# First-layer attention: three pairs of PSUM banks, one projection bank emptied by a copy, and a held TensorE order

## The chip, the cores and the metric

The kernel runs on one core of one Trainium2 chip. Its metric is the device time of one execution in microseconds (us): the median of three runs before the change is 1449.96 us (1449.54 to 1451.34). The engines of the core are TensorE (PE, with its weight loads shown apart as PEld), VectorE (DVE), ScalarE (ACT), GpSimd (POOL) and SyncE (SP), which issues the DMAs. Data lie in SBUF; TensorE writes its results to PSUM, which has eight banks of 512 float32 values for each of the 128 partitions. POOL takes no part in reading PSUM here.

## The reference, cut to what matters

Two layers over 1024 latent tokens and 256 context tokens, 1024 wide, 16 heads of 64. The first layer is windowed attention with rotary position and a sink logit for each head, a SiLU gate, an output projection and a LayerNorm; the second layer is a two-dimensional neighbourhood attention with the same frame. The change is in the first layer:

```
q, k, v, g = split(u @ w_in)             # u: tokens after adaLN; 4 key/value heads, 16 query heads
q, k = rope(q), rope(k)                  # latent tokens only
s = q . k / 8 over a block of 128 queries and its previous, own and next block, masked to |i-j| <= 128
p = softmax([s_window, s_context, sink])
o = p @ [v_window, v_context]
y = (o * silu(g)) @ w_out
h = layer_norm(sqrt(2) * h + gate * y)
```

Context queries attend to the context alone.

## The kernel before, in words

All products of float32 are kept exact enough by splitting operands into a high and a low part (`hi`, `lo`), so a projection of one 128-row weight tile onto 512 tokens is three matmuls (lines 208 to 210).

The first layer works on pairs of heads, p = 0 to 7. For each pair `subsA` lists 20 steps: ten blocks of 128 queries (8 of latents, 2 of context), each for two heads. Step k has these pieces of TensorE work:

- S (`qkA`, lines 694 to 716): the scores of step k + 3, four matmuls (two for context blocks) into one pair of PSUM banks, name `S_A`. VectorE adds the mask and takes the extreme (line 317, `m_A`), which frees that pair; ScalarE takes the exponential (324); VectorE inverts the sum (328); POOL normalises (329).
- T (`trA`, `sm_transpose`, line 336): up to five transpositions of step k's probabilities into another pair of banks, name `T_A`. ScalarE copies the high part (340), VectorE subtracts the low part (342), which frees that pair.
- V (`pvA_fn`, line 733): probabilities times values, in a first (high) and a second (low) half, into one bank, name `pvA`.

Before the change, PSUM is one pool: tag "big" with two pairs of banks, which S and T share, whichever is free, and tag "one" with four single banks, which the projections (`pj`) and `pvA` share.

While the attention of pair p runs, TensorE also computes the projections of the gate of pair p and of q of pair p + 1 (`proj_pieces`): for each, three chunks of tokens (512, 512, 256), each in eight pieces of three matmuls into one bank `pj`. At a chunk's last piece the bank is read by `evac`. For the gate (`g_evac`) that is a tanh on ScalarE (line 277) and a product on VectorE (278). For q (`rope_evac`) it is, for the two latent chunks, a shuffle (469) and a product with the cosine (470) on VectorE, a product with the sine on POOL (471), a sum on VectorE (472) into the one buffer "ra", and then for each of two heads a ScalarE cast (659) and a VectorE subtraction (660) that read "ra". The context chunk of q is stored from the bank itself by lines 659 and 660.

`merge` interleaves the two lists by their costs: it takes a projection piece whenever the projections' share done is not ahead of the attention's, so at the start of a pair (both zero) it takes a projection piece. `att_steps` sets the order of pieces within a step: T, S, V. This is the order in which the program is traced. A planner then gives each engine its order: it takes what is ready first in its own model of time, by priority; `lift(n)` raises the priority of what it encloses, and `keep_in_program_order` ties an instruction behind the one traced before it on its engine, without a wait.

Around it: `k_load` brings the keys of a group of two pairs as two tiles, with three buffers in all; q of pair 0 is computed alone before the attention (line 808); pair 7 has no q to fill with, and takes the output weights and the first output product (lines 824 to 848). Between them run the dot products of a modulation row (`dot_half`).

Of the kernel before, what the change touches and what calls it, by code (L numbers as in the profile page):

```python
# [19 lines left out]
P = 128  # L20
# [15 lines left out]
AHEAD_B, LIFT_B = 3, 40  # L36
BARE_B = 108
# [45 lines left out]
def build(tc, i, out):  # L83
    nc = tc.nc
    mm = nc.tensor.matmul
# [104 lines left out]
    def proj_pieces(j0, u, chunks, evac):  # L190
# [4 lines left out]
        def piece(ci, t0, n, kq):  # L195
# [18 lines left out]
            return (3 * 0.425 * n, run)  # L214
# [69 lines left out]
    def merge(att, fill, lead=0.0):  # L284

        ta = sum(a[0] for a in att) or 1.0
        tf = sum(f[0] for f in fill)
        ia = jf = 0
        ca = cf = 0.0
        while ia < len(att) or jf < len(fill):  # L290
            need = att[ia][2] if ia < len(att) and len(att[ia]) > 2 else 0
            if jf < len(fill) and (ia == len(att) or jf < need or cf - lead <= ca * (tf - lead) / ta):
                cf += fill[jf][0]
                fill[jf][1]()
                jf += 1
            else:
                ca += att[ia][0]
                att[ia][1]()
                ia += 1
# [31 lines left out]
    def sm_transpose(s, order, pt, hl, name):  # L331
# [3 lines left out]
        for k, src in enumerate(order):  # L335
            nc.tensor.transpose(tp[:, k * P : (k + 1) * P], s.t[:, src * P : (src + 1) * P], ident)  # L336
# [264 lines left out]
    def dot_half(h, j):  # L601
        def run():
# [13 lines left out]
            o = ap_.tile([P, 512], F32, tag="ra", bufs=1, name="gj")  # L616
# [29 lines left out]


# [45 lines left out]

    def qkA(k):
        p, b, h = subsA[k]
        q = qA[2 * p + h]
        sc = psbig(f"S_A{k}")
        ql = q[:, b * P : (b + 1) * P]
        n = len(tilesA(b)) * P - 256
        for l in range(2):  # L700
            kk = kA[p // 2, l]
            if n:
                t0 = tilesA(b)[0] * P
                mm(sc[:, 512 - n : 512], ql, kk[:, t0 : t0 + n], start=l == 0, stop=l == 1)
            mm(sc[:, 512:768], ql, kk[:, S:T], start=l == 0, stop=l == 1)  # L705
# [103 lines left out]
    px, px_st = pool("attA2", "right")  # L809
# [529 lines left out]
```

## Time and profile before

| what | value |
|---|---|
| median of three runs | 1449.96 us (1449.54 to 1451.34) |
| the profiled execution, its own time | 1450.25 us |
| its span, first to last instruction | 1448.5 us |
| granted TensorE clock, mean | 0.994 |
| TensorE busy | 1393.6 us, 96% |
| VectorE, ScalarE, POOL busy | 988.8, 733.9, 631.7 us |
| first S of the first layer | 98.1 us |
| last V of the first layer | 588.6 us |

The page gives for each engine the time in which it ran instructions. A row of a group names the line, the engine, the operation, what is written and read, and the count, then busy time and mean duration in ns, then the idle time of the engine before these instructions and what ended it. A row of waits says which engine, tile and line waited, for which engine, tile and line, and then the total in us, the number of waits and the longest. A timeline row gives the start in us from the start of the span, the duration, the engine and the instruction, with how many like it follow in the group (x5).

### The profile page before, as it was taken

The page shows a single profiled execution, that of the slowest core. Times are in us where ns is not written, and L with a number is a line of the kernel's source. Part 1 is how long each engine was busy: PE and PEld are TensorE (multiplying, and loading weights), DVE is VectorE, ACT ScalarE, POOL GpSimd, SP SyncE. Part 2 cuts the span into 40 slices and gives each one's busy share as a digit, 9 for nine tenths or more (in the row PEclk, how much of TensorE's full clock was granted, in tenths as well). Part 3 has the DMA queues.
Part 4 walks back from the last instruction along what each step waited for, and adds up shares of the span by engine and source line. Part 5 has one row for each costly group of instructions (what it writes and reads, how often), then busy time and mean ns, then how long its engine had stood idle before and what let it go on. Part 6 is the DMA issues. An engine that isn't in the chain of part 4 may idle for free. (4 is left out here: it accounts for less than half of the span.)

```text
span 1448.5 us, 25148 instructions
## 1 busy us (share of the span) xinstructions
PE 1393.6 (96%) x8815; PEld 1217.2 (84%) x8816; DVE 988.8 (68%) x2216; ACT 733.9 (51%) x1561; POOL 631.7 (44%) x779
## 2 busy tenths in 40 slices
PE   8998999999999999999999999999999999998995
PEld 5887888888888888788888899888988898887775
DVE  4658887878888789566423766555565565667698
ACT  4336776677676778332222545554454444557310
POOL 0326666666666657233301333333233333336664
PEclk9999999999999999999999999999999999999998
DMA  9472114123222124434278565565555564384353
GB/s 369 172 227 85 60 48 131 45 77 101 68 70 62 56 67 131 133 129 136 75 216 230 156 195 152 150 166 146 168 147 152 146 182 140 102 207 151 114 133 93
DMA packets 117229, 195.05 MB, mean 135 GB/s; under 512 B 9328, under 2 KB 57840, under 8 KB 117104
## 3 DMA queue, kind: packets, MB, share of 16 engines
q1 hardware_dynamic: 117104, 193.45, 44.4%
q8 instruction: 70, 1.15, 0.3%
q14 instruction: 55, 0.45, 0.1%
HBM read 141.51 MB, written 51.90 MB: 134 GB/s over the span
## 5 line engine op out<-in xcount | busy, mean ns | idle before, releaser
L329 POOL TENSOR_SCALAR s_B<-s_B,rs_B 128x640 f32<-128x640 f32 (+1 forms) x128 | 101.1, 790 | 298.0 <-DVE rs_B L328 243.9
L208 PE MATMUL pj<-uBh,wh 128*128 128x512 f32 (+1 forms) x448 | 176.0, 393 | 0.0
L209 PE MATMUL pj<-uBl,wh 128*128 128x512 f32 (+1 forms) x448 | 170.3, 380 | 0.0
L210 PE MATMUL pj<-uBh,wl 128*128 128x512 f32 (+1 forms) x448 | 170.1, 380 | 0.0
L324 ACT ACTIVATE s_B<-s_B,m_B 128x640 f32<-128x640 f32 (+1 forms) x128 | 102.9, 804 | 131.2 <-DVE m_B L317 131.1
L324 ACT ACTIVATE s_A<-s_A,m_A 128x641 f32<-128x641 f32 (+2 forms) x160 | 119.5, 747 | 88.7 <-DVE m_A L317 73.7
L164 POOL TENSOR_TENSOR wl<-wr,wh 128x512 fp32r<-128x512 f32 x64 | 87.7, 1370 | 162.1 <-ACT wh L162 139.8
L329 POOL TENSOR_SCALAR s_A<-s_A,rs_A 128x640 f32<-128x640 f32 (+2 forms) x160 | 126.8, 793 | 58.0 <-DVE rs_A L328 55.7
L317 DVE CUSTOM_DVE_ANT_0 s_A<-S_A,msk,nsk 128x640 f32<-128x640 f32 (+2 forms) x160 | 123.6, 774 | 34.1 <-PE S_A L705 17.7
L342 DVE TENSOR_TENSOR pt_B<-T_B,pt_B 128x640 fp32r<-128x640 f32 (+1 forms) x128 | 100.9, 788 | 61.0 <-ACT pt_B L340 60.6
L208 PE MATMUL pj<-uAh,wh 128*128 128x512 f32 (+1 forms) x384 | 140.0, 365 | 0.0
L209 PE MATMUL pj<-uAl,wh 128*128 128x512 f32 (+1 forms) x384 | 137.8, 359 | 0.0
L210 PE MATMUL pj<-uAh,wl 128*128 128x512 f32 (+1 forms) x384 | 137.5, 358 | 0.0
L342 DVE TENSOR_TENSOR ptl_A<-T_A,pth_A 128x640 fp32r<-128x640 f32 (+2 forms) x160 | 114.0, 713 | 15.3 <-PE pvA L733 7.1
L336 PE MATMUL T_A<-ident,s_A 128*128 128x128 f32 x672 | 101.1, 275 | 12.2 <-DVE m_A L317 8.9
L336 PEld LDWEIGHTS T_A<-ident,s_A 128*128 128x128 f32 x672 | 77.2, 140 | 40.2 <-issue 16.7
L340 ACT CAST pt_B<-T_B 128x640 fp32r<-128x640 f32 (+1 forms) x128 | 84.3, 658 | 47.6 <-PE T_B L336 46.6
L317 DVE CUSTOM_DVE_ANT_0 s_B<-S_B,bias 128x640 f32<-128x640 f32 (+1 forms) x128 | 100.4, 784 | 10.5 <-PE S_B L1036 9.7
L340 ACT CAST pth_A<-T_A 128x640 fp32r<-128x640 f32 (+2 forms) x160 | 96.4, 603 | 16.8 <-PE T_A L336 14.1
L210 PEld LDWEIGHTS pj<-uBh,wl 128*128 128x128 f32 x448 | 84.3, 188 | 16.6
L336 PE MATMUL T_B<-ident,s_B 128*128 128x128 f32 x608 | 88.7, 275 | 9.9 <-DVE pt_B L342 5.0
L242 PE MATMUL pv<-wh,uBh 128*128 128x256 f32 x320 | 92.8, 291 | 3.1 <-ACT wh L162 3.1
(219 smaller groups left out, 3883.6 us busy)
## 6 DMA issues: line engine op xcount, KB each, us to landing
kB<-kdB SPq DMA_DIRECT2D x64, 320.0 KB, 5.2
gw<-in_wadaT SPq DMA_DIRECT2D x48, 256.0 KB, 2.8
vdB<-st SPq DMA_DIRECT2D x20, 512.0 KB, 3.2
vB<-vdB SPq DMA_DIRECT2D x16, 640.0 KB, 4.7
wada<-in_wadaC SPq DMA_DIRECT2D x16, 512.0 KB, 9.6
kdB<-st SPq DMA_DIRECT2D x16, 512.0 KB, 3.0
qdB<-st SPq DMA_DIRECT2D x16, 512.0 KB, 3.5
qB<-qdB SPq DMA_DIRECT2D x32, 256.0 KB, 4.7
```

What stands on the lines that cost most here:

```text
L164: e.tensor_tensor(lo, r, f32(hi), ALU.subtract)
L208: mm(pt[:, :n], hi[:, sl], rh, start=kt == 0, stop=False)
L209: mm(pt[:, :n], hi[:, sl], rl, start=False, stop=False)
L210: mm(pt[:, :n], lo[:, sl], rh, start=False, stop=kt == KT - 1)
L242: mm(pt, lh, hi[:, sl], start=kt == 0, stop=False)
L317: nc.vector.tensor_tensor_reduce(outp, sc, in1, scale, init if init is not None else 3e38, ALU.add, ALU.min, accum_out=s.m)
L324: nc.scalar.activation(s.t[:, :n], s.t[:, :n], AF.Exp, bias=s.m, scale=-1.0, accum_out=s.sum)
L329: nc.gpsimd.tensor_scalar(s.t[:, : s.w], s.t[:, : s.w], s.rs, 1.0, ALU.mult, ALU.mult)
L336: nc.tensor.transpose(tp[:, k * P : (k + 1) * P], s.t[:, src * P : (src + 1) * P], ident)
L340: nc.scalar.copy(pt.hi[:, :n, hl, :], tv)
L342: nc.vector.tensor_tensor(pt.lo[:, :n, hl, :], tv, f32(pt.hi[:, :n, hl, :]), ALU.subtract)
```

## The change

Six edits, all around the first layer:

1. PSUM becomes a sequence of three pools: as before up to the first projections (two pairs, four singles), then for the first layer three pairs and two singles, one for `pj` and one for `pvA`, then two pairs and four singles again after the first output block. Pairs are taken strictly in turn by the traced order, each its own tag with one buffer, in all three pools.
2. The projections of q and of the gate are emptied by a copy on ScalarE, with the priority raised by `LIFT_PJ` = 40: q into "ra" (all three chunks, the context chunk too), the gate into its own tile `gA`. The rest of the work then reads the copy.
3. In `merge`, after the last piece of a first-layer chunk no projection piece is taken until attention pieces of cost 1700 have been.
4. From pair 0 up to and without pair 7 every matmul and transposition is tied behind the one traced before it.
5. For the first two steps of pairs 2, 4 and 6 the scores are issued in two parts: the part with the high keys at its place, the part with the low keys at the end of the second step.
6. The dot products write their unused result to "rb" instead of "ra", and the first output product of pair 7 takes the third pair (`big2`) instead of two single banks; from there the pairs in turn are two.

```
+LIFT_PJ = 40
+GAP_PJ = 1700.0
...
-    mm = nc.tensor.matmul
+    pinned = []
+    def pin(ins):
+        if pinned:
+            tc.keep_in_program_order(ins)
+    def mm(*a, **kw):
+        pin(nc.tensor.matmul(*a, **kw))
...
-    ps = es.enter_context(tc.tile_pool(name="ps", bufs=1, space=PSUM))
-    def psbig(name):
-        return ps.tile([P, 1024], F32, tag="big", bufs=2, name=name)
-    def psone(name):
-        return ps.tile([P, 512], F32, tag="one", bufs=4, name=name)
+    class Banks:
+        def open(self, name, pairs, ones):
+            self.st = ExitStack()
+            self.ps = self.st.enter_context(tc.tile_pool(name=name, bufs=1, space=PSUM, reuse_waits="tile"))
+            self.pairs, self.ones, self.n = list(range(pairs)), ones, 0
+        def big(self, name):
+            t = self.pairs[self.n % len(self.pairs)]
+            self.n += 1
+            return self.ps.tile([P, 1024], F32, tag=f"big{t}", bufs=1, name=name)
+        def one(self, name):
+            if self.ones == 4:
+                return self.ps.tile([P, 512], F32, tag="one", bufs=4, name=name)
+            return self.ps.tile([P, 512], F32, tag=name[:2], bufs=1, name=name)
+    banks = Banks()
+    banks.open("ps0", 2, 4)
+    psbig, psone = banks.big, banks.one
...
-            return (3 * 0.425 * n, run)
+            return (3 * 0.425 * n, run, GAP_PJ) if kq == 7 and j0 < NA else (3 * 0.425 * n, run)
...
-    def g_evac(pl, g):
+    def g_evac(pl, g, free=False):
         def evac(pt, t0, n):
+            if free:
+                pt, src = g[:, t0 : t0 + n], pt
+                with lift(LIFT_PJ):
+                    nc.scalar.copy(pt, src[:, :n])
             th = pl.tile([P, 512], F32, tag="ra", bufs=1, name="th")
...
-        ca = cf = 0.0
+        ca = cf = hold = 0.0
...
-            if jf < len(fill) and (ia == len(att) or jf < need or cf - lead <= ca * (tf - lead) / ta):
+            if jf < len(fill) and (ia == len(att) or jf < need or (ca >= hold and cf - lead <= ca * (tf - lead) / ta)):
                 cf += fill[jf][0]
                 fill[jf][1]()
+                if len(fill[jf]) > 2:
+                    hold = ca + fill[jf][2]
                 jf += 1
...
-    def rope_evac(store, pl, bufs):
+    def rope_evac(store, pl, bufs, free=False):
         def evac(pt, t0, n):
+            if t0 < S or free:
+                a = pl.tile([P, 512], F32, tag="ra", bufs=bufs, name="ra")
+            if free:
+                with lift(LIFT_PJ):
+                    nc.scalar.copy(a[:, :n], pt[:, :n])
+                pt = a
             if t0 >= S:
                 store(pt[:, :n], t0, n)
                 return
-            a = pl.tile([P, 512], F32, tag="ra", bufs=bufs, name="ra")
...
-            o = ap_.tile([P, 512], F32, tag="ra", bufs=1, name="gj")
+            o = ap_.tile([P, 512], F32, tag="rb", bufs=1, name="gj")
...
+    banks.st.close()
+    banks.open("psA", 3, 2)
...
-        return proj_pieces(pos["Aq", p], uA, CHUNKS, rope_evac(q_store(p), ap_, 1))
+        return proj_pieces(pos["Aq", p], uA, CHUNKS, rope_evac(q_store(p), ap_, 1, True))
...
-            g_evac(ap_, gA[p])(pt, t0, n)
+            g_evac(ap_, gA[p], True)(pt, t0, n)
...
     def qkA(k):
+        qk_part(k, 0)
+        if not (k >= 40 and k % 40 < 2):
+            qk_part(k, 1)
+    def qk_part(k, l):
...
+        if l == 0:
+            scA[k] = psbig(f"S_A{k}")
+        sc = scA[k] if l == 0 else scA.pop(k)
...
     merge([], qprojA(0))
     px, px_st = pool("attA2", "right")
+    pinned.append(True)
     for p in range(8):
-        att = [x for row in rowsA[p * 20 : (p + 1) * 20] for x in row]
+        rows_p = [list(row) for row in rowsA[p * 20 : (p + 1) * 20]]
+        if p == 7:
+            pinned.clear()
+        elif p % 2 == 0 and p:
+            late = range(p * 20, p * 20 + 2)
+            rows_p[1] += [(270.0, lambda k=k: qk_part(k, 1), 0) for k in late]
+        att = [x for row in rows_p for x in row]
...
-                yA0.extend(psone(f"yA0_{nh}") for nh in range(2))
+                banks.pairs = [0, 1]
+                y = banks.ps.tile([P, 1024], F32, tag="big2", bufs=1, name="yA0")
+                yA0.extend(y[:, sl] for sl in HALVES)
...
+        if b == 0:
+            banks.st.close()
+            banks.open("psB", 2, 4)
```

More of the change, by code (lines that the diff above doesn't have):

```diff
@@ L335, in sm_transpose @@
         for k, src in enumerate(order):
-            nc.tensor.transpose(tp[:, k * P : (k + 1) * P], s.t[:, src * P : (src + 1) * P], ident)
+            pin(nc.tensor.transpose(tp[:, k * P : (k + 1) * P], s.t[:, src * P : (src + 1) * P], ident))
         tv = tp[:, : n * P].rearrange("p (k q) -> p k q", k=n)
@@ L848, in build @@
             merge(att[-6:], [])
+    pinned.clear()
     px_st.close()
@@ L1241, in build @@
             dma(grid_rows(out, b)[:, :, sl], z[:, sl])
+    banks.st.close()
     ob_st.close()
```

18 lines of the change are left out of this document (9 added, 9 removed).

## The prediction

> **What bounds the kernel now.** I read the page first: TensorE's share of the span and the granted clock.
>
> ```profile
> span 1448.5 us, 25148 instructions
> ...
> PE 1393.6 (96%) x8815; PEld 1217.2 (84%) x8816; DVE 988.8 (68%) x2216; ACT 733.9 (51%) x1561; POOL 631.7 (44%) x779
> ```
>
> TensorE is busy nearly all the time. The profiled execution took 1450.25 us, 0.29 above the median of 1449.96; my sum starts at 1450.25. Next comes the table by stage of the changed stretch: pair 0 of the heads, pairs 1 to 6, and pair 7 with its tail. After the stretch and its length stand the busy us (and instructions) of TensorE, its weight loads, VectorE, ScalarE and POOL, then the granted clock, DMA share and GB/s.
>
> ```profile
> 98.00:158.00 60.00, 55.07 (x355) 47.72 (x353) 47.97 (x114) 39.47 (x89) 38.04 (x54) 1.00 0.35 99
> 158.00:525.00 367.00, 356.66 (x2318) 312.93 (x2319) 300.31 (x732) 255.81 (x584) 239.74 (x346) 1.00 0.24 74
> 525.00:595.00 70.00, 65.24 (x412) 56.45 (x411) 56.24 (x129) 51.26 (x110) 41.22 (x59) 1.00 0.34 106
> ```
>
> The shown idle time of TensorE is 4.93 + 10.34 + 4.76 = 20.0 us. The waits of TensorE say what ends it; the first three rows are of the whole kernel, the fourth of 525 to 595 us alone.
>
> ```profile
> PE T_A L336 <- DVE m_A L317: 8.9, 16, 1.6
> PE S_A L704 <- DVE ptl_A L342: 5.1, 7, 1.2
> PE S_A L705 <- DVE ptl_A L342: 1.8, 6, 0.3
> ```
> ```profile
> PE T_A L336 <- DVE m_A L317: 3.2, 5, 1.5
> ```
>
> A transposition (T) needs its scores from POOL, yet it waits for the minimum that VectorE takes of other scores (L317); scores (S) need only q and k, yet wait for VectorE's read of a transposition (L342). So both wait for a pair of banks: S and T share two. The timeline at the boundary from pair 1 to pair 2 of heads shows two such waits, and three things more.
>
> ```profile
> 216.11 0.28 PE L208 MATMUL pj<-uAh,wh 128*128 128x256 f32 x1
> 216.23 0.28 PE L209 MATMUL pj<-uAl,wh 128*128 128x256 f32 x1
> 216.34 0.28 PE L210 MATMUL pj<-uAh,wl 128*128 128x256 f32 x1
> 216.46 0.40 PE L208 MATMUL pj<-uAh,wh 128*128 128x512 f32 x1
> 216.70 0.40 PE L209 MATMUL pj<-uAl,wh 128*128 128x512 f32 x1
> 216.93 0.40 PE L210 MATMUL pj<-uAh,wl 128*128 128x512 f32 x1
> 217.48 0.41 PE L336 MATMUL T_A<-ident,s_A 128*128 128x128 f32 x2 [0.15 <-DVE m_A L317]
> 218.56 0.39 PE L704 MATMUL S_A<-kA,qA 128*128 128x256 f32 x1 [0.67 <-DVE ptl_A L342]
> ```
>
> First, a 128x512 matmul is drawn 0.40 long but the next starts 0.23 later, so each wait hides about 0.16 us more than its row says. The three rows hold 15.8 us in 29 waits, truly about 15.8 + 29 x 0.16 = 20.4. Second, the gate projection of pair 2 (216.46, 512 wide) follows directly on the last matmul of the query projection (216.34, 256 wide): no attention lies between. The merge makes it so at the start of each pair, because with both sums at zero its test takes a projection piece first. Third, that costs nothing now, since the projections have several banks.
>
> **The change, part by part.**
>
> *Third pair.* The waits of 98 to 525 us are (15.8 - 3.2) + 24 x 0.16 = 16.4, those of the tail 4.0, of which the third pair lives only in the first half: 2.0. With three pairs in turn a pair comes back after one and a half steps instead of about one. VectorE works 300.31 of 367 us (82%), so some lateness stays: I take 17 of the 18.4 as gone, with 10 as the lower bound (VectorE stays the last to answer).
>
> *The copies.* Each projected chunk gets a ScalarE copy: 8 x 3 for q, 8 x 3 for the gates. The nearest rows are the reads of the same bank for the second layer and for q's context columns.
>
> ```profile
> L932 ACT CAST st<-pj 128x512 fp32r<-128x512 f32 x16 | 9.4, 586 | 18.5 <-PE pj L210 13.0 <-issue 4.2 <-ACT otmp L1073 1.0
> L659 ACT CAST qA<-pj 64x256 fp32r<-64x256 f32 x16 | 5.8, 361 | 3.9 <-DVE qA L660 3.9
> L472 DVE TENSOR_TENSOR ra<-ra,rb 128x512 f32<-128x512 f32 x20 | 18.1, 903 | 1.1 <-POOL rb L471 0.8
> L470 DVE TENSOR_TENSOR ra<-pj,cos 128x512 f32<-128x512 f32 x16 | 10.8, 672 | 0.0
> ```
>
> 32 x 0.586 + 16 x 0.361 = 24.5 us of ScalarE, which is busy 255.81 of 367 (70%) and goes to about 76%: covered by TensorE's own work, so nothing by itself. VectorE's cosine product now reads two SBUF operands, like L472: up to 0.23 more on 16 instructions, 3.7 us, also covered while VectorE has 18% free; without that cover it would add at most those 3.7.
>
> *One projection bank, inside a pair of heads.* The hold of 1700 puts four attention pieces (4 x 545) between chunks, 35 times over pairs 0 to 6. Four full pieces are about 0.6 us each, 2.3 together; with the short blocks at a pair's end 1.5. The bank must be read meanwhile. A late case of today:
>
> ```profile
> 226.69 0.39 PE L210 MATMUL pj<-uAh,wl 128*128 128x512 f32 x1
> ```
> ```profile
> 228.39 0.59 ACT L277 ACTIVATE th<-pj 128x512 f32<-128x512 f32 x1
> ```
>
> ScalarE came 1.31 us after the bank was complete (227.08) and would free it 0.16 + 1.31 + 0.59 = 2.1 us after TensorE could have gone on. So most handovers fit and some miss by a few tenths: I take 2 us in all; bounds 0 and 10 (0.3 each).
>
> *One projection bank, at the boundaries.* Here no piece lies between (216.34 to 216.46), the order is held, and the first piece of the next pair needs the bank. Its emptying copy writes the buffer "ra", of which there is one, and the previous chunk of q still uses it until its last subtraction:
>
> ```profile
> 217.37 0.69 DVE L660 TENSOR_TENSOR qA<-ra,qA 64x512 fp32r<-64x512 f32 x1
> ```
>
> That ends at 218.06, 1.6 us after TensorE reaches the boundary. Before, the 256-wide chunk did not touch "ra". Add the copy (0.36) and a hop (0.1): 2.1. The previous chunk's work starts a copy later (up to 0.7), but meets less traffic; I take 2.0 at each of the six boundaries from pair 0 to 6, 12 us. Bounds: 0.6 (hop, 0.16 and copy alone, "ra" free in time), 4 us, and 2.8, 17 us. Queued behind the waiting matmul stand the transposition and the scores of 217.48 and 218.56, so softmax starves too; what it gains is that their own waits vanish, and these are among the 17.
>
> *Start.* q of pair 0 runs before any attention, its three chunks back to back on the one bank.
>
> ```profile
> 92.05 0.28 PE L208 MATMUL pj<-uAh,wh 128*128 128x256 f32 x1
> ...
> 94.80 0.28 PE L210 MATMUL pj<-uAh,wl 128*128 128x256 f32 x1
> 94.92 0.40 PE L208 MATMUL pj<-uAh,wh 128*128 128x512 f32 x1
> ```
> ```profile
> 92.26 0.74 DVE L469 STREAM_SHUFFLE rb<-pj 128x512 f32<-128x512 f32 x1
> 93.03 2.39 DVE L660 TENSOR_TENSOR qA<-ra,qA 64x512 fp32r<-64x512 f32 x2
> ```
>
> The first handover costs a copy and its hops, 1.0. The second chunk's copy waits for "ra" until the first chunk's subtractions end (93.03 + 2.39 = 95.42 now; 94.4 at the 0.69 of the row at 217.37), so the 256-wide chunk starts near 95.1 instead of 93.1: 2.0. Its own copy waits for the second chunk's rotation, which begins at 95.1 and takes a shuffle, the sine product on POOL, a sum, two ScalarE casts and two subtractions, the first of these beside the second cast:
>
> ```profile
> L471 POOL TENSOR_TENSOR rb<-rb,sin 128x512 f32<-128x512 f32 x20 | 27.6, 1378 | 34.1 <-DVE rb L469 34.1
> L659 ACT CAST qA<-ra 64x512 fp32r<-64x512 f32 x32 | 19.8, 619 | 8.2 <-DVE ra L472 7.8
> ```
>
> 0.74 + 1.38 + 0.7 + 2 x 0.62 + 0.69 and some 0.5 of hops make 5.2, with 0.46 for copy and hop 100.8; TensorE is through its 24 matmuls (0.12 each) at 98.0: 2.8. Sum 6; bounds 2 and 8.
>
> *Clock.* Two waits of the second layer show what stalls of this length do.
>
> ```profile
> 728.83 0.80 PE L242 MATMUL pv<-wh,uBh 128*128 128x256 f32 x2 [3.15 <-ACT wh L162]
> ```
> ```profile
> 1332.72 1.30 PE L336 MATMUL T_B<-ident,s_B 128*128 128x128 f32 x5 [2.11 <-POOL gB L1077]
> ```
> ```profile
> 728.40:731.80 3.40, 2.97 (x14) 2.97 (x15) 1.90 (x7) 0.38 (x1) 0.00 (x0) 0.50 0.42 131
> 1329.20:1332.60 3.40, 1.41 (x12) 1.20 (x10) 2.84 (x5) 1.55 (x3) 2.44 (x3) 1.00 0.39 123
> 1332.60:1336.00 3.40, 3.28 (x13) 2.92 (x13) 1.23 (x3) 2.67 (x7) 2.79 (x4) 0.50 0.49 193
> ```
>
> After 3.15 and after 2.11 us of idling the granted clock was 0.50 for 3.4 us, worth up to 1.7 us each. The stalls of 2.0 to 2.8 lie at this edge; I let two of the eight trip it, 3 us; bounds 0 and 11. [...]
>
> *Split scores, other layers.* Halving the scores of k = 40, 80, 120 and their partners issues the same matmuls. The second half needs the k tile whose load (median below) is issued after the last scores of the old pair.
>
> ```profile
> kA<-kdA SPq DMA_DIRECT2D x16, 320.0 KB, 5.0
> ```
>
> The boundary stall covers that landing; without it the matmul would wait about 1.5 us, three times. In the second layer S and T now alternate strictly over two pairs where a free one was taken; TensorE idles little there, so 0, with -1 and +4 as bounds.
>
> The sum: 1450.25 - 17 + 6 + 12 + 2 + 3 = 1456.
>
> **The rivals.**
>
> *The boundary is cheap, and the kernel gets faster.* If the rotation of q's second chunk is done when TensorE reaches the boundary, each stall is 0.6, the start 3, handovers 1, no clock loss: 1450.25 - 18.4 + 4 + 3 + 1 = 1440. For it: the rotation needs 5.2 us plus a first copy, 0.6, and TensorE takes 216.46 - 210.70 = 5.8 between the two chunks, by the last matmul of the earlier one:
>
> ```profile
> 210.47 0.40 PE L210 MATMUL pj<-uAh,wl 128*128 128x512 f32 x1
> ```
>
> Against it: with VectorE's other work it takes until 218.06 today. It decides at "ra" being free within about 0.5 us of the last q matmul. Chance 0.35.
>
> *Gain and price cancel.* Boundaries of 1.3 (8), start 5, handovers 2, one clock drop: 1450.25 - 17 + 8 + 5 + 2 + 1.6 = 1450. Chance 0.12.
>
> *Every boundary trips the clock.* Eight drops of 1.6 instead of two: 1456 + 9.6 = 1466. For it the row of 1332.6; against it the many waits up to 1.6 us at clock 1.00. Chance 0.08.
>
> *The third pair does not do what it says.* VectorE at 82% plus its dearer reads stays last, and only 8 of the 17 go: 1465. Against it: the waits are few and short, up to 1.6, and a pair now stays away longer than that. Chance 0.05.
>
> **How the numbers follow.** The forecast, slower at 1456, has 0.40. A change under 0.2% (2.9 us) can't be told from none. Faster: the first rival, 0.35, and a little of the second, 0.36 together; within 0.2%: 0.12; slower: 0.40 + 0.08 + 0.05, less the forecast's near edge, 0.52. The forecast's own range is 1450 to 1464. For 8 in 10 the range must hold most of the first rival and half of the last two: 1437 to 1467.
>
> **What would show it.** Right: in the profile after, T and S rows no longer wait for L317 and L342; new rows "PE pj <- ACT" for the copy's line, some 2 us each, at the six boundaries, with the 256-wide q copy on ScalarE ending just before; two waits between 87 and 102 us on the same tile; single 3.4 us windows at clock 0.50 inside the first layer. Wrong: if the pj waits stay under 1 us at the boundaries, the first rival holds; if T and S still wait for VectorE by over 8 us, the third pair's term falls; if the second layer's windows move by more than 4 us, the alternating pairs there matter and I have missed it.

## The result and the profile after

The changed kernel takes 1620.66 us (median of four, 1619.68 to 1621.47) against 1449.89 us (1449.54 to 1451.34) for the kernel before on the same chip: a ratio of 1.1175, with an interval of 1.1156 to 1.1195. It is 171 us slower; the prediction said 6. Below, line numbers are those of the changed kernel, where all matmuls show the line of their helper, L96; the others lie some 30 to 55 above those of the kernel before: transpositions L370, the mask with its extreme L351, the exponential L358, the probabilities' high and low part L374 and L376, the projections' copy L503, pvA's two readers L795 and L796.

The page of the changed kernel:

```profile
span 1617.9 us, 25174 instructions
...
PE 1449.2 (90%) x8816; PEld 1262.2 (78%) x8816; DVE 1011.0 (62%) x2216; ACT 762.2 (47%) x1609; POOL 639.1 (40%) x779
```

The matmuls are as many as before; TensorE's share falls from 96% to 90%. The span grows by 169.4 us. The first S starts at 110.3 us (98.1 before) and the last V at 759.8 (588.6): this stretch, called the stage from here on, takes 649.5 us in place of 490.5. So 159.0 us come from the stage and 12.2 from the start. From the last V to the end it is 858.1 against 859.9: the second layer loses nothing.

The table of busy times for the stage, first of the changed kernel and then of the kernel before (columns: stretch and length; busy us and instructions of TensorE, its weight loads, VectorE, ScalarE, POOL; granted clock; DMA share; GB/s):

```profile
110.00:760.00 650.00, 523.33 (x3064) 457.51 (x3063) 421.52 (x966) 368.35 (x819) 323.26 (x456) 0.91 0.19 57
```
```profile
98.00:589.00 491.00, 470.97 (x3057) 412.15 (x3056) 401.94 (x969) 344.66 (x778) 317.83 (x457) 1.00 0.26 81
```

TensorE's idle time goes from 20.0 to 126.7 us, and the same matmuls take 52.4 us longer. That is 106.7 + 52.4, the whole 159. The second part is nearly all the clock: by the trace's clock records TensorE ran at half clock for 114.8 us of this stage (and for 8.1 us ahead of it), and in the kernel before for none. Matmuls ran for 98.7 of the 114.8 us. At half clock the 128x512 matmuls of a projection start 0.43 us apart (244.16 and 244.59 us in the changed kernel), at full clock 0.23 (246.18 and 246.41), so about half of the 98.7, 49.4 us, is put down to the clock here; it is an estimate. All other engines are busy for a smaller share than before, so none of them is the bound by its load.

The waits of TensorE in the whole changed kernel (us in total, times, longest):

```profile
PE pvA L96 <- DVE otmp L796: 78.6, 32, 4.3
PE S_A L96 <- DVE ptl_A L376: 28.1, 38, 1.3
PE pj L96 <- ACT ra L503: 17.2, 9, 6.0
...
PE T_A L370 <- DVE m_A L351: 1.3, 4, 0.8
```

The largest is a row that the kernel before does not have and the prediction does not name: V waits for the bank of pvA until VectorE has summed the last contents out of it. What holds that sum up shows in the timeline of the changed kernel inside pair 1, some 24 us ahead of the boundary to pair 2 that the prediction looked at:

```profile
236.20 0.76 PE L96 MATMUL pvA<-ptl_A,vA 128*128 128x256 f32 x5
...
236.93 0.83 ACT L358 ACTIVATE s_A<-s_A,m_A 128x641 f32<-128x641 f32 x1
...
237.76 0.68 ACT L374 CAST pth_A<-T_A 128x640 fp32r<-128x640 f32 x1
...
238.46 0.37 ACT L795 COPY otmp<-pvA 64x256 f32<-64x256 f32 x1
...
238.50 0.80 DVE L376 TENSOR_TENSOR ptl_A<-T_A,pth_A 128x640 fp32r<-128x640 f32 x1
...
239.44 0.75 DVE L351 CUSTOM_DVE_ANT_0 s_A<-S_A,msk,nsk 128x512 f32<-128x512 f32 x1
...
240.12 0.69 DVE L510 TENSOR_TENSOR ra<-ra,cos 128x512 f32<-128x512 f32 x1
240.32 0.72 ACT L358 ACTIVATE s_A<-s_A,m_A 128x513 f32<-128x513 f32 x1 [1.49 <-DVE m_A L351]
240.72 0.41 DVE L796 TENSOR_TENSOR otmp<-pvA,otmp 64x256 f32<-64x256 f32 x1
...
241.16 0.37 ACT L795 COPY otmp<-pvA 64x256 f32<-64x256 f32 x1
...
241.25 0.69 DVE L512 TENSOR_TENSOR ra<-ra,rb 128x512 f32<-128x512 f32 x1
...
241.97 0.42 DVE L796 TENSOR_TENSOR otmp<-pvA,otmp 64x256 f32<-64x256 f32 x1
...
242.53 1.41 PE L96 MATMUL pvA<-pth_A,vA 128*128 128x256 f32 x5 [3.24 <-DVE otmp L796]
...
243.74 0.63 PE L96 MATMUL pj<-uAh,wh 128*128 128x512 f32 x1
```

The last matmul into pvA ends at 236.96. Four instructions read the bank: a ScalarE copy, a VectorE sum, and both again for the other head, 0.37 + 0.41 + 0.37 + 0.42 = 1.57 us together. They end at 242.39, 5.4 us later. The first copy stands behind an exponential and a cast, its sum behind a subtraction, a mask and the rotation's cosine product, the second copy behind an exponential that itself waits 1.49 us, the second sum behind the rotation's sum. Meanwhile the held order lets TensorE do nothing that comes after this V. The matmuls that follow at 243.74 take 0.63 us in place of 0.39: the clock has fallen, to a mean of 0.54 from 242.40 to 245.80.

And the wait feeds itself. The scores of the next steps stand behind the waiting V, so VectorE runs dry in turn. VectorE's wait for scores, in the stage of the changed kernel and in that of the kernel before:

```profile
DVE s_A L351 <- PE S_A L96: 111.3, 69, 6.9
```
```profile
DVE s_A L317 <- PE S_A L705: 17.7, 40, 2.5
```

### The profile page after: what moved, and what is told of

It reads as the page before. It is cut to its first block, busy times and chain, and to the rows that moved or that the text cites. A ratio compares the mean times of both kernels' runs of the same rounds, so it can differ in the third digit from the quotient of the medians.

```text
span 1617.9 us, 25174 instructions
## 1 busy us (share of the span) xinstructions
PE 1449.2 (90%) x8816; PEld 1262.2 (78%) x8816; DVE 1011.0 (62%) x2216; ACT 762.2 (47%) x1609; POOL 639.1 (40%) x779
## 5 line engine op out<-in xcount | busy, mean ns | idle before, releaser
L351 DVE CUSTOM_DVE_ANT_0 s_A<-S_A,msk,nsk 128x640 f32<-128x640 f32 (+2 forms) x160 | 123.8, 774 | 138.4 <-PE S_A L96 111.3
L96 PE MATMUL pj<-uBh,wh 128*128 128x512 f32 (+1 forms) x448 | 176.2, 393 | 0.0
L96 PE MATMUL pj<-uAh,wh 128*128 128x512 f32 (+1 forms) x384 | 155.6, 405 | 17.2 <-ACT ra L503 17.2
L96 PE MATMUL pj<-uBl,wh 128*128 128x512 f32 (+1 forms) x448 | 170.7, 381 | 0.0
L96 PE MATMUL pj<-uBh,wl 128*128 128x512 f32 (+1 forms) x448 | 170.5, 381 | 0.0
L358 ACT ACTIVATE s_A<-s_A,m_A 128x641 f32<-128x641 f32 (+2 forms) x160 | 119.4, 746 | 102.6 <-DVE m_A L351 95.2
L358 ACT ACTIVATE s_B<-s_B,m_B 128x640 f32<-128x640 f32 (+1 forms) x128 | 102.9, 804 | 126.3 <-DVE m_B L351 125.8
L191 POOL TENSOR_TENSOR wl<-wr,wh 128x512 fp32r<-128x512 f32 x64 | 84.0, 1312 | 172.0 <-ACT wh L189 140.7
L374 ACT CAST pth_A<-T_A 128x640 fp32r<-128x640 f32 (+2 forms) x160 | 96.5, 604 | 110.7 <-PE T_A L370 105.0
L96 PE MATMUL pj<-uAl,wh 128*128 128x512 f32 (+1 forms) x384 | 148.3, 386 | 0.0
L96 PE MATMUL pj<-uAh,wl 128*128 128x512 f32 (+1 forms) x384 | 147.6, 384 | 0.0
L96 PE MATMUL pvA<-pth_A,vA 128*128 128x256 f32 x336 | 67.8, 335 | 83.2 <-DVE otmp L796 78.6
L96 PE MATMUL S_A<-kA,qA 128*128 128x384 f32 (+1 forms) x576 | 116.8, 319 | 28.1 <-DVE ptl_A L376 28.1
L376 DVE TENSOR_TENSOR pt_B<-T_B,pt_B 128x640 fp32r<-128x640 f32 (+1 forms) x128 | 101.0, 789 | 61.9 <-ACT pt_B L374 61.5
L96 PEld LDWEIGHTS pvA<-pth_A,vA 128*128 128x128 f32 x336 | 57.3, 230 | 94.8 <-issue 89.6
L376 DVE TENSOR_TENSOR ptl_A<-T_A,pth_A 128x640 fp32r<-128x640 f32 (+2 forms) x160 | 113.4, 712 | 26.4 <-PE pvA L96 12.8
L96 PEld LDWEIGHTS S_A<-kA,qA 128*128 128x128 f32 x576 | 89.1, 192 | 43.4 <-DVE ptl_A L376 39.1
L370 PE MATMUL T_A<-ident,s_A 128*128 128x128 f32 x672 | 106.4, 285 | 8.8 <-POOL s_A L363 7.3
L374 ACT CAST pt_B<-T_B 128x640 fp32r<-128x640 f32 (+1 forms) x128 | 84.5, 660 | 59.7 <-PE T_B L370 59.0
L351 DVE CUSTOM_DVE_ANT_0 s_B<-S_B,bias 128x640 f32<-128x640 f32 (+1 forms) x128 | 100.5, 785 | 14.0 <-PE S_B L96 8.1
```

The source lines that it names most:

```text
L96: pin(nc.tensor.matmul(*a, **kw))
L191: e.tensor_tensor(lo, r, f32(hi), ALU.subtract)
L351: nc.vector.tensor_tensor_reduce(outp, sc, in1, scale, init if init is not None else 3e38, ALU.add, ALU.min, accum_out=s.m)
L358: nc.scalar.activation(s.t[:, :n], s.t[:, :n], AF.Exp, bias=s.m, scale=-1.0, accum_out=s.sum)
L370: pin(nc.tensor.transpose(tp[:, k * P : (k + 1) * P], s.t[:, src * P : (src + 1) * P], ident))
L374: nc.scalar.copy(pt.hi[:, :n, hl, :], tv)
```

## The experiments

Each is one profiled and timed execution; the kernel before, beside them, took 1447.3 to 1449.0 us, so a difference of some 4 us says nothing. "Stage" is the time from the first S to the last V, "half clock" the part of the stage at a granted clock of 0.5, from the clock records. In seven of them (a1, b4, c4, d2, d4, e1, e2) the output product behind the stage waits 7 to 9 us for a bank that the step before it still reads (the row of e1 below shows it), which is a matter of how the banks behind the stage were laid out in them. So parts are compared by the stage, which leaves that out.

| kernel | label | us | stage | against before | half clock |
|---|---|---|---|---|---|
| before | | 1449.9 | 490.5 | | 0 |
| changed | | 1620.7 | 649.5 | +159.0 | 114.8 |
| changed, planner's order | a2 | 1509.3 | 552.0 | +61.5 | 34.1 |
| changed, pvA's readers raised | a3 | 1558.7 | 590.5 | +100.0 | 66.1 |
| changed, pvA emptied early | b1 | 1528.2 | 559.7 | +69.2 | 25.9 |
| b1 and the boundary mended | b2 | 1521.1 | 553.8 | +63.3 | 20.5 |
| b2, gate's product on POOL | d3 | 1527.9 | 561.5 | +71.0 | 27.3 |
| b1, pairs taken as free | c1 | 1518.0 | 545.1 | +54.6 | 36.0 |
| changed, two pairs, pvA two banks | a1 | 1593.9 | 613.8 | +123.3 | 49.6 |
| changed, no copies | c3 | 1664.0 | 685.8 | +195.3 | 139.7 |
| changed, banks of before | c4 | 1529.1 | 562.3 | +71.8 | 27.3 |
| before, held order | a4 | 1479.7 | 522.0 | +31.5 | 27.3 |
| before, hold | e1 | 1474.7 | 507.0 | +16.5 | 10.2 |
| before, copies | b4 | 1486.0 | 518.5 | +28.0 | 10.2 |
| b4, copies not raised | e2 | 1483.4 | 515.6 | +25.1 | 15.9 |
| b4, gate's product on POOL | d4 | 1490.8 | 523.3 | +32.8 | 6.8 |
| before, three pairs and two singles | b3 | 1514.5 | 548.4 | +57.9 | 25.8 |
| before, one bank each for pj and pvA | c2 | 1511.6 | 552.5 | +62.0 | 17.1 |
| before, one bank for pj alone | d1 | 1505.9 | 546.0 | +55.5 | 37.5 |
| before, one bank for pvA alone | d2 | 1475.7 | 508.1 | +17.6 | 3.4 |

**Is it the bank of pvA, and the held order?** The first theory: pvA's readers are late, and the held order makes TensorE wait for them. Against it stood the held order by itself. Run a1 gave pvA a second bank at the third pair's cost, a2 let the planner order TensorE again, a3 raised the readers' priority, b1 also put both copies ahead of both sums.

```
a1   banks.open("psA", 3, 2) -> 2 pairs;  tag "pv": bufs=2;  scores whole
a2   -    pinned.append(True)
a3   +                with lift(100):   # around copy and sum, for each head
b1   +            with lift(100):
     +                for h, hs in enumerate(hss):
     +                    nc.scalar.copy(tmp[hs], pv[64:128, :, h, :])
     +                for h, hs in enumerate(hss):
     +                    nc.vector.tensor_tensor(tmp[hs], pv[0:64, :, h, :], tmp[hs], ALU.add)
```

> The changed kernel with the probabilities-times-values products on two banks in turn and S and T on two pairs instead of three (so the split scores are undone too); copies, hold and held order stay. Theory A (the one bank of pvA, emptied late, is the loss): the 78.6 us of pvA waits fall under 5 us, the clock recovers with them, time 1460 to 1500. Rival H (the held order is the loss, whatever the banks): over 1580. Rival J (the projection bank): pj waits of some 17 us stay, so over 1465.

> The changed kernel without the held order; banks, copies and hold stay. Theory A: the planner can put projection pieces into the waits for the pvA bank, but not all: pvA waits halve, time 1480 to 1560. Rival H: at or under 1456, since only the order is the loss.

> The changed kernel with the four instructions that empty the pvA bank raised in priority by 100, nothing else. Theory A: the pvA waits fall from 78.6 to 20 to 40 us, the half-clock windows halve, time 1500 to 1550. Rival H: still over 1590, since the waits move to S and T.

> The changed kernel with the pvA bank emptied by both ScalarE copies first and then both VectorE sums, all raised by 100. Theory A (one late-emptied pvA bank, and the clock that falls behind its waits): pvA waits fall from 78.6 (32.4 with the raise alone) under 20 us, time 1500 to 1545. Rival (the held order itself): stays at 1558 or above, S and T waits grow by what pvA loses.

TensorE's waits in a1:

```profile
PE T_A L370 <- DVE ptl_A L376: 52.4, 50, 2.5
PE pj L96 <- ACT ra L503: 33.2, 9, 6.1
PE T_A L370 <- DVE rs_A L362: 32.1, 21, 3.4
```

In a3 and then in b1:

```profile
PE pvA L96 <- DVE otmp L797: 32.4, 27, 2.4
```
```profile
PE S_A L96 <- DVE ptl_A L376: 36.5, 43, 2.0
PE pj L96 <- ACT ra L503: 27.4, 9, 6.0
PE pvA L96 <- DVE otmp L798: 12.2, 21, 1.2
```

a2 gives back 111 us and b1 92, both where the theory put them; a3 gives 62 and misses its range by 9 us. Reading pvA's bank early, with no bank and no order of TensorE changed, takes away more than half of the loss, so this wait is shown to be the largest part of it. a2's gain is not a further one: with the planner's order the same waits fall from 78.6 to 11.6 us, so they cost what they do only while the order is held. The 89.8 us that b1 takes off the stage can be followed: TensorE idles 56.4 us less, since pvA's waits fall by 66.4 while those of S and pj grow, and its matmuls take 33.4 us less, with the half clock down from 114.8 to 25.9. a1 missed by 94 us, at a time that rivals H and J had given: the waits of pvA for the sum went, but two pairs strictly in turn brought 84.5 us of waits of T, and pj's grew from 17.2 to 33.2. A bank given back to pvA was taken from another tile that needed it as much; how much of this is the missing pair and how much the strict turn, a1 does not tell.

**What each edit costs alone.** The rest of the loss was still to be split: the held order (a4), the copies (b4), the hold (e1), the banks (b3 with the third pair, c2 without it), and the change with all but the banks (c4).

```
a4   +    pinned.append(True)      # and mm, transpose tied, as in the change; nothing else
b4   rope_evac(..., True), g_evac(..., True);  banks, hold and order as before
e1   +                if len(fill[jf]) > 2:
     +                    hold = ca + fill[jf][2]     # no copies or held order; banks as before
b3   banks.open("psA", 3, 2), strictly in turn, scores split;  no copies, hold or held order
c2   banks.open("psA", 2, 2), as free;  tags "pj" and "pv" bufs=1;  no copies, hold or held order
c4   banks.open("psA", 2, 4), as free;  scores whole;  the rest of the change stays
```

Only a4 is cut from the kernel before. All others here are cut from the changed kernel and keep its three pools and the dot products' buffer "rb" (of edits 1 and 6), so their prices hold whatever these two cost; no run has them alone.

> The kernel before with the held order of pairs 0 to 6 alone; two pairs, four single banks, no copies. Theory A: 1445 to 1470. Rival H: over 1550.

> Banks as in the changed kernel (three pairs in turn, one bank each for pj and pvA), but no copies, no hold and no held order. Theory A: the waits for the single banks are there, pvA the larger, yet the planner fills part: 1470 to 1530. Rival (the third pair pays, the held order and the copies cost): under 1447, with S and T waits on VectorE under 8 us.

> The kernel before with the ScalarE copies of the q and gate chunks alone; two pairs and four single banks, planner's order, no hold. Prediction's term (covered, nothing): 1446 to 1454. Rival (VectorE's queue waits for the copies ahead of softmax work): over 1456, with more S and T waits on VectorE than the 15.8 us before.

> The kernel before (planner's order, two pairs as they come free, banks read in place, no hold, scores whole), with nothing changed but that pj has one bank and pvA has one bank in the first layer, in place of four that they share. Three pairs with those two singles alone took 1514.5 us. Theory A (the single banks are what costs): 1490 to 1530, TensorE's waits of 3 us and longer, on T_A for POOL and on pj and pvA, as with three pairs. Rival (it was the third pair that moved the planner's order): 1450 to 1465. Between them: both have a part.

> The changed kernel with the banks of the kernel before in the first layer (two pairs as they come free, four singles that pj and pvA share) and whole scores; copies, hold and the traced order stay. Theory A (each part costs by itself and the single banks most): the copies' 37 and the traced order's 31 add up, 1500 to 1530, no wait of pvA for the sum on VectorE over 3 us in all, and so the banks are 90 to 120 of the 171 us. Rival C (with order and copies together the cost is there whatever the banks): over 1570.

> The kernel before with the hold alone: after each projected chunk no projection piece until attention pieces of cost 1700 have been; banks, readers and the planner's order as before. Theory N (the kernel before stands on one order, and any other order of the same work costs, as the held order's 31 and the copies' 37 did): 1470 to 1490. Rival (the hold moves a few pieces and costs nothing by itself): 1446 to 1455.

One wait of TensorE in c4, and one in e1, which lies behind the stage:

```profile
PE S_A L96 <- DMA kA<-kdA: 20.3, 5, 5.1
```
```profile
PE yA L96 <- DVE z L967: 9.3, 1, 9.3
```

By the stage, the held order costs 31.5 us, the copies 28.0, the hold 16.5, the single banks 62.0. The first three add to 76.0, and c4, which has them all, shows 71.8: they add up, and if they do so exactly, the pools and "rb", twice in the 76.0 and once in c4, cost about 4, no more than the noise. In that frame the banks cost 159.0 - 71.8 = 87.2 (by the times 91.6, in the range written for them), and b3, c2 and c4 came out within the ranges of the theory of the single banks. The third pair seems worth little: from c2 to b3 the stage moves from 552.5 to 548.4. But b3 also takes its pairs strictly in turn and splits the scores, so the pair by itself is not measured. The copies' run went to the rival (over 1456). a4 came out 10 us above its range, and far from the other theory's 1550; e1 came out in theory N's range, but of its 27 us in time 9.3 are the output product's wait, so the hold itself is cheaper than that range says. In c4 the fifth edit shows its use by its absence: with whole scores and a held order, 20.3 us of waits for the k tiles.

**Which of the two single banks?** Under the planner's order, one bank for pj and three for pvA, and the other way round.

```
d1   -  bufs=1      +  bufs=1 if name[:2] == "pj" else 3     # against c2
d2   -  bufs=1      +  bufs=3 if name[:2] == "pj" else 1
```

> The kernel before (planner's order, two free pairs, banks read in place) with one bank for pj and three for pvA; one each took 1511.6 us. Theory V (the bank of pvA, emptied by four instructions that nothing raises, is what costs): 1450 to 1470, waits of pj for VectorE's ra and shuffle under 15 us, most of it at the start. Theory J (the bank of pj, held by a whole rotation, costs most): 1490 to 1515.

> The kernel before with three banks for pj and one for pvA. Theory V: 1490 to 1515, waits of pvA for the sum on VectorE 10 to 30 us. Theory J: 1450 to 1470. If both this one and the other come out near 1480, each single costs a half.

Here the theory that carried the first group fails. d1 costs 55.5 us of the stage and d2 17.6: where the planner may reorder, it is the projections' single bank that costs, as theory J said (d2 lies 6 us above J's range). The waits of d1 hardly name it; its one row for pj is nearly all the start:

```profile
PE pj L96 <- DVE ra L506: 6.1, 2, 5.6
```

What shows is other work made late: in the stage TensorE idles 46.3 us in place of 20.0, and its matmuls take 29 us longer, of which the half clock (33.9 us of matmuls in it) explains 17 by the same estimate. A likely reason, not shown, is that the planner puts the matmuls of pj where it takes the bank to be free, so that the loss appears under other names. In the held order, where V may not be moved, the wait for the bank of pvA costs most (b1 takes 89.8 of the 159.0 us off the stage); no run gives pj its banks back there.

**Does VectorE set the pace?** With the copies, VectorE's operations get dearer. The groups of VectorE in the stage of the kernel before, and of b4:

```profile
L660 DVE TENSOR_TENSOR qA<-ra,qA 64x512 fp32r<-64x512 f32 x30 | 24.9, 831 | 4.7 <-ACT qA L659 4.2
...
L472 DVE TENSOR_TENSOR ra<-ra,rb 128x512 f32<-128x512 f32 x14 | 10.5, 750 | 0.8 <-POOL rb L471 0.7
L470 DVE TENSOR_TENSOR ra<-pj,cos 128x512 f32<-128x512 f32 x14 | 9.4, 670 | 0.0
```
```profile
L699 DVE TENSOR_TENSOR qA<-ra,qA 64x512 fp32r<-64x512 f32 x30 | 31.1, 1035 | 1.6 <-ACT qA L698 0.7
L508 DVE TENSOR_TENSOR ra<-ra,rb 128x512 f32<-128x512 f32 x15 | 15.1, 1005 | 2.6 <-POOL rb L507 2.3
...
L506 DVE TENSOR_TENSOR ra<-ra,cos 128x512 f32<-128x512 f32 x15 | 14.3, 954 | 0.0
```

VectorE's busy time in the stage grows by 24.5 us, from 401.94 (above) to this, in b4:

```profile
98.00:618.00 520.00, 479.69 (x3061) 416.08 (x3061) 426.45 (x973) 369.37 (x828) 332.06 (x459) 0.99 0.25 76
```

Both are 82% of their stretch, which suggested that VectorE sets the pace. d3 and d4 take the gate's product off it; e2 takes the copies' priority away; c3 leaves the copies out of the change, c1 frees the pairs from their turn.

```
d3, d4  -  nc.vector.scalar_tensor_tensor(g, th, 1.0, pt, ALU.add, ALU.mult)
        +  nc.gpsimd.tensor_tensor(th, th, pt, ALU.mult)
        +  nc.gpsimd.tensor_tensor(pt, th, pt, ALU.add)
e2      LIFT_PJ = 40 -> 0
c3      rope_evac(..., True), g_evac(..., True) -> without True
c1      f"big{t}", bufs=1 -> "big", bufs=len(self.pairs)     # three in the first layer; with b1's edit
```

> The changed kernel with pvA emptied early, the hold at the start of each pair, and the context chunk of q in rb (1521.1 us); and the gate's product taken from VectorE to POOL, as a product and a sum of two SBUF operands. Theory P (VectorE sets the pace of the attention): some 20 us of VectorE's work go, the waits of S_A for VectorE fall from 45 to under 30 us and the time to 1495 to 1512. Rival (a chain of steps and its hops sets the pace, not VectorE's load): no change within 5 us, or slower, as POOL's normalisation stands in a longer queue.

> The kernel before with the copies alone (1486.0 us), and the gate's product on POOL as in the run beside it. Theory P: VectorE has about the load of the kernel before, and the time comes back to 1448 to 1468. Rival (the copies cost through the planner's order or through ScalarE): 1478 or more. Below 1447 it would beat the kernel before.

> The kernel before with the copies alone (1486.0 us), their priority not raised. Theory S (the raised copies stand ahead of the exponential and of the high part of the probabilities in ScalarE's queue): 1450 to 1468, and the 18.9 us of S_A waiting for ptl_A fall under 12. Rival N (the copies lengthen the rotation and change the order of all engines, raised or not): 1478 to 1495.

> The changed kernel (1620.7 us) without the copies: the projections' bank is read in place by the rotation and by the tanh and the product of the gate; three pairs in turn, the single banks, the hold and the traced order stay. Theory A (the copies load VectorE, +37 us when they stand alone): 1575 to 1605, pvA's wait for the sum on VectorE still the largest, under 70 us. Rival B (with a single bank the copy is needed: without it each chunk holds TensorE until shuffle, product or tanh have read it): the waits of pj grow from 17 us to over 50 and the time is over 1620.

> The changed kernel with the bank of pvA emptied early (1528.2 us), and the three pairs of banks taken by whichever is free instead of strictly in turn. Theory T (the strict turn makes the scores wait for the pair that a late transposition still holds): the waits of S_A for VectorE's ptl_A, 36.5 us in 43 times, fall under 15, and the time under 1512. Theory Q (VectorE is late as an engine; whichever pair is asked for, its reader stands in VectorE's queue): the waits of S_A and T_A for VectorE together stay at 30 or more and the time within 1518 to 1540.

The pace theory is not borne out. In d4 VectorE is busy 15.7 us less than in b4, and the stage is 4.8 longer:

```profile
98.00:623.00 525.00, 479.46 (x3061) 414.09 (x3061) 410.75 (x949) 368.90 (x828) 379.83 (x507) 0.99 0.25 76
```

POOL pays for it: it is busy 47.8 us longer than in b4, and the two operations take it 42.5 us on the 512-wide chunks (rows of POOL's groups in d4) and 11.8 us on the others:

```profile
L308 POOL TENSOR_TENSOR th<-th,gA 128x512 f32<-128x512 f32 x16 | 21.7, 1357 | 2.0 <-ACT th L306 2.0
L309 POOL TENSOR_TENSOR gA<-th,gA 128x512 f32<-128x512 f32 x16 | 20.8, 1300 | 0.9
```

By the times, d3 is 6.8 us slower than b2, and d4 is 4.8 us slower than b4. Why the move does not pay, beyond POOL's longer work, no run here shows.

The priority isn't the cause either (e2 is 2.6 us better, within the noise). So for the copies' 28 us the priority is excluded and no cause is shown. VectorE's load is not excluded altogether, since d4 lengthens POOL's queue by more than it shortens VectorE's. It stays open; another candidate is that each rotation gets a step longer and stands in two engines' queues until it is done. In c3, without the copies, the change is 43 us slower still: with a single bank they do help. Theory A missed there; rival B's time came true but not its reason, for pj's waits are 26.6 us in two rows, not over 50, and pvA took the most:

```profile
PE pvA L96 <- DVE otmp L796: 113.0, 32, 6.6
...
PE pj L96 <- DVE qA L703: 19.4, 7, 5.8
```

c1 agrees with each theory by half. The waits of S for the transposition's pair, 36.5 us in b1, are gone, as the theory of the strict turn said, but the time fell by 10 only, to the edge of the other theory's range, since pvA's rose from 12.2:

```profile
PE pvA L96 <- DVE otmp L796: 37.9, 24, 2.8
```

**The boundary.** b2 adds to b1 a hold at the start of each pair and gives q's context chunk the buffer "rb".

```
-        ca = cf = hold = 0.0
+        hold = GAP_PJ if att and fill and len(fill[7]) > 2 and lead == 0.0 else 0.0
-                a = pl.tile([P, 512], F32, tag="ra", bufs=bufs, name="ra")
+                a = pl.tile([P, 512], F32, tag="ra" if t0 < S else "rb", bufs=bufs, name="ra")
```

> The previous kernel, and the hold applied at the start of each pair of heads too, and q's context chunk copied into the buffer rb instead of ra. Theory of the boundary: the pj waits inside the attention (6 to 17 us) go, those of the start shrink by the last of three, time 10 to 25 us under the previous kernel. Rival: under 3 us difference, since other waits take their place.

The waits of pj go from 27.4 us to 5.1, all that is left at the start, and the first S starts at 103.9 instead of 110.2. But the time falls by 7.1 only, between the theory's range and the rival's: S waits 44.6 us in place of 36.5, and of the 12.2 us that the start and the stage gain together, 5.1 are lost behind the stage, for a cause that stays open. Of this kernel's PE waits:

```profile
PE S_A L96 <- DVE ptl_A L377: 44.6, 50, 2.2
...
PE pj L96 <- ACT ra L504: 5.1, 2, 4.5
```

## Why the prediction was wrong

The direction held; the size was off by 165 us. That the direction held is in part luck: the start and the boundaries, which were to make the kernel slower, came to 17 of the 171 us. Step by step:

- **What bounds the kernel.** TensorE, at 96% with 20 us idle: right. The prediction then asked only which of these 20 us would go and which stalls come at pj. It did not ask what else the four single banks had served.
- **The bank of pvA: the step that failed.** The prediction's part on "one projection bank" prices pj's handovers and leaves pvA's at nothing, without saying so, though the kernel's description names both. Its readers were in the traces of before, in four instructions that alternate between two engines and that nothing raises. Measured: 78.6 us of waits, and 92 us of time gained when the bank is emptied early.
- **The held order.** It was the condition of the boundary's price and had no price of its own. Measured 31.5 us alone; in the whole change, with the banks, 97.5 (649.5 - 552.0).
- **Third pair, -17.** The waits of T for the mask went, from 8.9 to 1.3 us. Those of S for a transposition's pair grew from 6.9 to 28.1, where the prediction's sign of "over 8 us" for a fallen term stood. Beside the single banks, three pairs in turn with split scores gain 4 us over two as they come free; c1 shows what the turn costs in the held order, 14.6 us of the stage (559.7 - 545.1).
- **Copies, 0.** Measured 28, with the pools and "rb" in it. Their ScalarE time was right in size (from 344.66 to 369.37, 24.7 against 24.5), VectorE's share was not: 24.5 against "at most 3.7", since the sums and subtractions stretched too. That the time was "covered" is what failed; by what, is open.
- **Handovers inside a pair, 2, with the hold.** The hold costs 16.5 without a single bank, again with the pools and "rb" in it.
- **Boundaries, +12, and start, +6.** The sizes came out half and double; the mechanism was right at the boundaries and in part at the start. The rows of the changed kernel from 115 to 700 us, and from 85 to 115:

```profile
PE pj L96 <- ACT ra L503: 6.0, 6, 1.2
```
```profile
PE pj L96 <- ACT ra L503: 11.2, 3, 6.0
```

  Six boundaries at 1.0 us, not 2.0. At the start it is 11.2 us in three waits, so that the first S came 12.2 later: 4.5, 0.7 and 6.0, where the prediction had 1.0, 2.0 and 2.8. The first copy stood behind ScalarE's stores of the values, and the last behind a rotation whose casts came after an instruction of ScalarE that waited 3.6 us for a DMA (tile gh); neither was in the sum. When b1 took the pvA waits away, the six boundaries rose from 6.0 to 16.3 us, 2.7 each: part of their price had been hidden behind pvA.
- **Clock, +3, two drops.** By the estimate above 49.4 us in the stage; from the start of q's projection on there were 25 drops. That stalls of 2 to 3 us are followed by half clock was foreseen; but eight stalls were counted, where there were over eighty.
- **Split scores, 0, and the second layer, 0.** The second layer was right. What the split itself costs, no run shows; but the prediction put the split's worth at three waits of 1.5 us; without it c4 waited 20.3 us and a4, with the held order alone, this:

```profile
PE S_A L92 <- DMA kA<-kdA: 12.2, 4, 3.5
```

- **The rivals.** That the third pair doesn't do what it says, with VectorE last, was nearest to S's waits and was priced at 9 us. That every boundary trips the clock had the right kind of loss at the wrong place. None had a wait of pvA, and the range of 30 us held only what had been named.

## What to carry to other kernels

When a pool of buffers is divided into named ones, list every tile that used the pool, with all readers of each and where these stand in their engines' queues: a buffer is free when its last reader is done, here 5.4 us for 1.57 us of work. In this kernel the held order turned a late reader into idle time of the engine (78.6 us of TensorE's waits for pvA's bank) and of what it feeds (VectorE's waits for scores, 111.3 us in place of 17.7), and waits that were taken away came back in part at other tiles (in b1 those of S rose from 28.1 to 36.5 us and those of pj from 17.2 to 27.4), so a mended wait is to be judged by the time and not by its row. Price each edit of a combined change also as if it stood alone; here four of them (the single banks, the held order, the copies, the hold) lost time without the others, and even the hold, which adds no work, came with 16.5 us.

## What was not expected of the hardware

The clock fell far more often than foreseen, 25 times against two. Two neighbouring stretches of the changed kernel, at a drop:

```profile
508.40:511.80 3.40, 1.39 (x10) 0.95 (x9) 2.79 (x8) 2.55 (x7) 1.87 (x3) 0.99 0.00 0
511.80:515.20 3.40, 1.36 (x6) 1.39 (x7) 3.31 (x8) 1.60 (x3) 2.58 (x3) 0.50 0.02 5
```

TensorE ran matmuls for 1.39 of the 3.4 us ahead of it. The clock records of the changed kernel show the half clock in pieces of 3.41 us; in the 3.41 us ahead of each of the 25 drops of its first layer TensorE ran matmuls for 0.15 to 1.44 us. Ahead of one drop in c3 it was 1.78:

```profile
768.20:771.60 3.40, 1.78 (x12) 1.29 (x11) 3.05 (x8) 3.30 (x9) 2.21 (x5) 1.00 0.01 3
771.60:775.00 3.40, 2.81 (x13) 2.81 (x14) 2.32 (x6) 2.89 (x7) 1.97 (x3) 0.50 0.37 115
```

Counted in such pieces, from 80 us to the last V of the changed kernel, every one at full clock with 1.44 us of matmuls or less was followed by half clock, and none with 1.55 or more was; in c3 the drop came after 1.78, so the two traces show no common edge. So the stalls that left TensorE 1.44 us or less of a piece cost their own length and then, by the estimate of 49.4 us in 114.8, some 1.5 us more for each 3.41 us at half clock; 14 of the 25 drops lasted one such piece and 11 two.

The other is the stretching of VectorE's operations: the rotation's sum reads two operands in SBUF before and after, with no edit of its own, and took 750 ns in the stage of before and 1005 ns in that of b4, with the copies. In these two kernels the longer ones are those beside POOL. Two of these sums in b4, the first beside an operation of POOL that had begun before it, the second with POOL idle when it begins:

```profile
227.71 1.29 POOL L189 TENSOR_TENSOR wl<-wr,wh 128x512 fp32r<-128x512 f32 x1
228.12 1.43 DVE L508 TENSOR_TENSOR ra<-ra,rb 128x512 f32<-128x512 f32 x1
```
```profile
343.43 0.68 DVE L508 TENSOR_TENSOR ra<-ra,rb 128x512 f32<-128x512 f32 x1
```

In the stage of before and of b4 the sums that begin with POOL idle take 0.68 us (7 of 14 before, 6 of 15 in b4); those that begin beside a running operation of POOL take 0.82 us on average before and 1.22 in b4, 0.69 to 1.74. In the stage of the changed kernel it is not so: eight sums that begin beside a running operation of POOL take 0.67 to 0.78 us, six that begin with POOL idle 0.69. The cosine product, while it read the bank in PSUM, took 0.66 to 0.68 us although POOL was at work at each of its 14 starts; with the copy in SBUF it takes 0.69 to 1.25 in b4, and in the stage of the changed kernel 0.69 in the six that begin with POOL idle and 0.69 to 1.24 in the eight beside it. So with the copy it could be longer beside POOL, where it had not been before. By what means, and beside which work of POOL, no run here shows.
